# A hybrid attention block on one core: four group-norm scalings go from VectorE to ScalarE, and a retention preparation's query products come ahead of its key transposes

## The chip, the cores and the metric

The kernel runs on one core of a Trainium2 chip. The metric is the time of one execution on the device in microseconds, the median of several runs. Five engines work side by side, each through its own list of instructions in a fixed order: TensorE (PE: matrix products and transposes), VectorE (DVE), ScalarE (ACT), GpSimd (POOL) and SyncE (SP, which here issues DMA transfers). An engine whose next instruction waits for a semaphore holds everything that stands behind it in its list.

## The reference, cut to what matters

Two layers of a block with three branches (retention, neighborhood attention, latent attention), a gated merge and an MLP, over 512 tokens x and 256 context tokens z of width 1024. The change lies in the retention. There are four heads in two pairs, keys and queries of 64, values of 128, chunks of 128 tokens, and two directions:

```
qx, kx, vx = retention_qkv(px[0], px[1], px[2], rope)      # q and k rotated, k scaled
scores = einsum(qc, kc) * decay_mat                        # inside a chunk
inner  = einsum(scores, vc)
kv     = einsum(kc * k_decay, vc)                          # the state, chunk by chunk
cross  = einsum(qc * q_decay, s_prev)
o      = inner + cross                                     # for each direction

def head_group_norm(o, gain):                              # over the 128 of a head
    mu, var = mean(o), mean(square(o - mu))
    return merge_heads((o - mu) * rsqrt(var + EPS)) * gain

y = silu(g_fwd) * head_group_norm(o_fwd) + silu(g_bwd) * head_group_norm(o_bwd)
```

## The kernel before

All products are of fp32 split into a high and a low part, so that one product is three matrix products (L435, L436, L437 in the helper `mm3`; L656 to L658 with the tokens as output rows). The high part is copied by ScalarE (`hi_of`, L386), the low part is the difference that VectorE takes (`lo_of`, L389). A weight (`wsp`) is split in the same way when it has arrived from memory.

The branches are Python generators. `Retention.prep(p2)` prepares one pair of heads: it rotates the keys (`rotated("rk")`), makes values for the first two token tiles, transposes the keys back to tokens and scales them (`kt`, `ktf`), makes the decay matrices `gm` and `qd` by Exp on ScalarE, rotates the queries (`rotated("rq")`), makes the other values (`values(2)`, `values(4)`), then the states. A rotation is a product of 24 or 48 matrix instructions, a copy out of PSUM by ScalarE (L1229, tile `ra`; L1240, tile `rz`), four DMAs that swap halves of the partitions (L1232, `rb<-ra`), and three operations of VectorE (L1233 to L1235), after which `ra` is the rotated tensor.

`Retention.run(p2)` then goes over the items of the pair, one for each head and block of 256 tokens: six items in the first layer (context included), four in the second, for each of two pairs, so 20 in all. An item has three steps: s0 makes scores (L684) and multiplies them by `gm` (L1364, `pf`, split by L386 and L389); s1 multiplies by values and states (L1388 into the PSUM tiles `pst`), adds up (L1391 ScalarE, L1392 VectorE, tile `ro`) and does the group norm; s2 transposes the result (L1413) and scales it (L1418, `ry`). The group norm of an item is four statistics (L1398, L1399), an addition (L1400), a power by GpSimd (L1401, `rs`), four scalings (L1404) and the gates (L1405, L1406):

```
pool.tensor_tensor(rs, rs, half, op=ALU.pow)
for i in range(4):
    v = ov[:, i // 2, i % 2]
    dve.tensor_scalar(v, v, mv[:, i, 0:1], rs[:, i : i + 1], op0=ALU.subtract, op1=ALU.mult)
```

What a generator yields as it goes is woven into the steps of the loop that runs at the time (`fill.feed`): `prep(0)` into the neighborhood attention, `prep(1)` into `run(0)`, the branch outputs into `run(1)`. Behind this a scheduler puts each engine's instructions into one fixed list from its own estimate of when operands are there. PSUM tiles of the long products (`pd`) rotate through three banks, so that a product into a bank starts only when the tile that had it before has been read out.

In the profiled execution the retention of pair 0, with `prep(1)` woven in, runs from about 604 to 682 us in the first layer and from 2006 to 2068 us in the second. The neighborhood attention with `prep(0)` lies ahead of each, pair 1 at about 780 to 890 and 2110 to 2172 us.

Of the kernel before, what the change touches and what calls it, by code (L numbers as in the profile page):

```python
# [8 lines left out]
F32 = mybir.dt.float32  # L9
F32R = mybir.dt.float32r  # L10
BF16 = mybir.dt.bfloat16
AF = mybir.ActivationFunctionType
ALU = mybir.AluOpType
# [296 lines left out]
def cost(columns):  # L310

    return columns / 2400.0
# [3 lines left out]
def block_kernel(ctx, tc, xT, zT, cond, wu, sp, bias, tab, out):  # L316
# [11 lines left out]
    small = ctx.enter_context(tc.tile_pool(name="small", bufs=4))  # L328
# [8 lines left out]
    def nm(s):  # L337
        count[0] += 1
        return f"{s}_{count[0]}"
# [4 lines left out]
    def sgl(s="s"):  # L344
        return sgls.tile([128, 512], F32, tag="sgl", name=nm(s))
# [36 lines left out]
    act, dve, pool, pe, sync = nc.scalar, nc.vector, nc.gpsimd, nc.tensor, nc.sync  # L382
# [21 lines left out]
    for l in range(DEPTH):  # L404
        t = const.tile([128, SP_N], F32, name=f"sp{l}")
# [173 lines left out]
    def new_tiles(n, nk):  # L579

        r = []
        while len(r) < nk:
            r += halves(dbl("t"), n)
        return r[:nk]
# [579 lines left out]
    class Retention:  # L1164
# [39 lines left out]
        def prep(self, p2):  # L1204

            l, need, lg = self.l, self.need, self.lg
# [6 lines left out]
            dm, qp = dbl("dist"), sgl("qpos")  # L1213
# [44 lines left out]

            yield values(0)

            kt = new_tiles(512, 6)
            for src, i0 in ((k32, 0), (kz32, 4)):
                nt = src.shape[-1] // 128
# [9 lines left out]
                    hi_of(t[:, :256], f)  # L1273
                    lo_of(t[:, 256:], f, t[:, :256])
                yield cost(512)

            gm = new_tiles(512, 2)
            for o in range(2):
                for dr in range(2):
                    c = 4 * dr + 2 * p2 + o  # L1280
                    act.activation(gm[o][:, 256 * dr : 256 * dr + 256], dist[:, 256 * dr : 256 * dr + 256], AF.Exp, scale=lg[:, c : c + 1])

                ends, cut_off = (t.rearrange("p (e n) -> p e n", n=128)[:, 0:4:3] for t in (gm[o], mask))
                pool.tensor_tensor(ends, ends, cut_off, op=ALU.mult)

            qd = sgl("qd")
            for dr in range(2):
                act.activation(qd[:, 256 * dr : 256 * dr + 256], qp[:, 256 * dr : 256 * dr + 256], AF.Exp, scale=self.lq[:, p2, dr : dr + 1])
            qx, qz, q32, _ = rotated("rq", 1.0, need, False)
            yield cost(24 * (768 if need else 512))  # L1290
            for i in (2, 4):
                yield values(i)

# [49 lines left out]
        def item(self, p2, o, c):  # L1343
# [25 lines left out]
            def s1():  # L1369
                qx, qz, kx, kz, vs, gm, sts, qc = self.state[p2]  # L1370
                prob = st["p"]
                ops = [bank_t().rearrange("p (c h v) -> p c h v", c=2, h=2) for _ in range(2)]
                for ct in range(2):
                    for dr in range(2):

                        if dr == 0:
                            terms = [(0, 128 * ct)] + ([(1, 256)] if ct == 1 else [])
                        else:
                            terms = [(1, 128 * ct)] + ([(0, 256)] if ct == 0 else [])
                        mms = []  # L1380
                        for kt_i, col in terms:
                            v = vs[2 * c + kt_i][:, 256 * o : 256 * o + 256]
                            mms += [(t[:, col : col + 128], v) for t in prob[dr]]
                        if c < 2:
                            sv = sts[0 if (c == 0) == (dr == 0) else 1][dr]
                            mms.append((qc[o][dr][:, c0 + 128 * ct : c0 + 128 * ct + 128], sv[:, 256 * o : 256 * o + 256]))
                        for n, (a, b) in enumerate(mms):
                            pe.matmul(ops[dr][:, ct], R(a), R(b), start=n == 0, stop=n == len(mms) - 1)  # L1388
                ov = st["ov"] = sgl("ro").rearrange("p (c t v) -> p c t v", c=2, t=2)
                for dr in range(2):  # L1390
                    act.activation(ov[:, :, dr], ops[dr][:, :, 0], AF.Copy)  # L1391
                    dve.tensor_tensor(ov[:, :, dr], ops[dr][:, :, 1], ov[:, :, dr], op=ALU.add)  # L1392

                mv = small.tile([128, 4, 2], F32, tag="mv", name=nm("mv"))
                st6 = small.tile([128, 4, 6], F32, tag="st6", name=nm("st6"))
                rs = small.tile([128, 4], F32, tag="rs", name=nm("rs"))
                for i in range(4):
                    dve.bn_stats(st6[:, i], ov[:, i // 2, i % 2])  # L1398
                    dve.bn_aggr(mv[:, i], st6[:, i])  # L1399
                dve.tensor_scalar(rs, mv[:, :, 1], EPS, 0.0, op0=ALU.add, op1=ALU.add)  # L1400
                pool.tensor_tensor(rs, rs, half, op=ALU.pow)  # L1401
                for i in range(4):
                    v = ov[:, i // 2, i % 2]
                    dve.tensor_scalar(v, v, mv[:, i, 0:1], rs[:, i : i + 1], op0=ALU.subtract, op1=ALU.mult)  # L1404
                dve.tensor_tensor(ov, ov, st["gt"], op=ALU.mult)  # L1405
                dve.tensor_tensor(ov[:, :, 0], ov[:, :, 0], ov[:, :, 1], op=ALU.add)  # L1406

# [475 lines left out]
```

## Time and profile before

| what | value |
|---|---|
| median of 3 runs | 2614.82 us (2610.67 to 2619.2) |
| the profiled execution's own time | 2613.25 us |
| its span on the core | 2611.4 us |
| mean granted TensorE clock | 0.983 |
| PE busy | 2523.3 us (97%) |
| DVE busy | 1771.6 us (68%) |
| ACT busy | 1140.0 us (44%) |
| POOL busy | 135.6 us (5%) |

Busy is the time in which an engine has an instruction running, not the time in which it is the one that others wait for. The clock is the share of full speed that was granted to TensorE. The shares are means over the whole span; the stages of the retention look otherwise, and the windows and waits among the rows below show them by themselves.

### The profile page before, as it was taken

Reading aid. Unit: us, or ns where it says so; the run is one execution under the profiler, and the core shown is the slowest. Engines: PE = TensorE matmul, PEld = TensorE weight load, DVE = VectorE, ACT = ScalarE, POOL = GpSimd, SP = SyncE. Lnnn points to the kernel's source line nnn. Section 1 sums busy time; section 2 is a strip of 40 time slices with the busy share of each in tenths; the row PEclk is TensorE's granted clock in tenths of the full one; section 3 lists DMA queues with packets and bytes.
Section 4 is the critical chain, followed back from the end, with each engine's and each line's share of the span. In section 5 each row is a group of like instructions: output and inputs, shape, how many; then the busy total and the mean of one; then the engine's idle time right before and its main releaser. Section 6 shows DMA issues by size and latency. Waiting matters only on the chain.

```text
span 2611.4 us, 40080 instructions
## 1 busy us (share of the span) xinstructions
PE 2523.3 (97%) x15346; PEld 2246.8 (86%) x15346; DVE 1771.6 (68%) x3492; ACT 1140.0 (44%) x2144; POOL 135.6 (5%) x121
## 2 busy tenths in 40 slices
PE   8999999998999999999999999999999899999997
PEld 7999998998888877888888878889898788988887
DVE  6566556787979875666556767665668768744457
ACT  2555555564323345322222446554555434732325
POOL 0101000111000000000000000010001000000000
PEclk9899999999999999999999999999999999999999
DMA  6222224534765633344444424323554456433333
GB/s 242 92 71 89 69 86 127 156 92 138 255 196 157 205 112 104 121 133 142 127 132 129 143 79 140 97 82 104 148 158 116 129 184 204 145 98 97 97 97 121
DMA packets 151316, 340.46 MB, mean 130 GB/s; under 512 B 18642, under 2 KB 58962, under 8 KB 151124
## 3 DMA queue, kind: packets, MB, share of 16 engines
q1 hardware_dynamic: 140756, 322.17, 40.1%
q10 hardware_dynamic: 10368, 15.73, 1.6%
q8 instruction: 121, 1.98, 0.3%
q14 instruction: 71, 0.58, 0.1%
HBM read 288.27 MB, written 36.45 MB: 124 GB/s over the span
## 4 chain that ended last, share of the span: by engine, by line
PE 79%; DVE 10%; issue 3%; ACT 3%; DMA 2%; POOL 1%; SPq 1%; POOLq 0%; DVEq 0%; ACTq 0%
PE pd L437 20%; PE pd L436 20%; PE pd L435 20%; PE pso L625 3%; PE pst L608 3%; PE pd L658 3%; PE pd L656 3%; PE pd L657 3%; DVE op L389 1%; PE pss L436 1%; PE pss L435 1%; PE pss L437 1%; DVE wsp L389 1%; PE pss L684 1%; ACT wsp L386 1%
## 5 line engine op out<-in xcount | busy, mean ns | idle before, releaser
L435 PE MATMUL pd<-op,wsp 128*128 128x512 f32 (+1 forms) x3080 | 1072.3, 349 | 26.5 <-ACT op L597 5.9
L437 PE MATMUL pd<-op,wsp 128*128 128x512 f32 (+1 forms) x3080 | 1064.4, 347 | 11.7 <-DVE wsp L389 11.7
L436 PE MATMUL pd<-op,wsp 128*128 128x512 f32 (+1 forms) x3080 | 1070.0, 348 | 2.5 <-DVE op L389 2.3
L435 PEld LDWEIGHTS pd<-op,wsp 128*128 128x128 f32 x3080 | 587.7, 191 | 101.0 <-ACT wsp L386 7.1
L437 PEld LDWEIGHTS pd<-op,wsp 128*128 128x128 f32 x3080 | 587.2, 191 | 84.3 <-DVE wsp L389 14.1
L436 PEld LDWEIGHTS pd<-op,wsp 128*128 128x128 f32 x3080 | 588.9, 191 | 72.2 <-DVE op L389 6.5
L386 ACT ACTIVATE wsp<-wraw 128x1024 fp32r<-128x1024 f32 x319 | 336.4, 1055 | 431.8 <-PE pd L437 303.4
L389 DVE TENSOR_TENSOR wsp<-wraw,wsp 128x1024 fp32r<-128x1024 f32 x319 | 388.6, 1222 | 174.9 <-ACT wsp L386 174.0
L656 PE MATMUL pd<-wsp,op 128*128 128x256 f32 x704 | 202.1, 287 | 1.7 <-DVE pr L766 1.6
L658 PE MATMUL pd<-wsp,op 128*128 128x256 f32 x704 | 200.6, 285 | 0.9 <-DVE wsp L389 0.9
L657 PE MATMUL pd<-wsp,op 128*128 128x256 f32 x704 | 200.4, 285 | 0.0
L1770 DVE TENSOR_TENSOR rl<-rl 128x256 f32<-128x256 f32 (+1 forms) x104 | 59.0, 567 | 150.6 <-ACT rl L1769 150.4
L389 DVE TENSOR_TENSOR pt<-pst,pt 128x512 fp32r<-128x512 f32 (+1 forms) x208 | 121.7, 604 | 44.2 <-ACT pt L386 42.0
L1769 ACT ACTIVATE rl<-pd 128x256 f32<-128x256 f32 (+1 forms) x104 | 51.8, 499 | 227.4 <-PE pd L437 227.2
L1784 DVE TENSOR_TENSOR t<-pd,t 128x512 f32<-128x512 f32 (+1 forms) x132 | 81.0, 617 | 89.9 <-PE pd L437 89.5
L656 PEld LDWEIGHTS pd<-wsp,op 128*128 128x128 f32 x704 | 136.3, 194 | 2.7 <-issue 1.8
L658 PEld LDWEIGHTS pd<-wsp,op 128*128 128x128 f32 x704 | 136.1, 193 | 1.5 <-DVE wsp L389 1.5
L657 PEld LDWEIGHTS pd<-wsp,op 128*128 128x128 f32 x704 | 136.4, 194 | 0.0
L386 ACT ACTIVATE pt<-pst 128x512 fp32r<-128x512 f32 (+1 forms) x208 | 105.2, 529 | 50.9 <-PE pst L608 37.6
L625 PE MATMUL pso<-pt,t 128*128 128x256 f32 x704 | 115.5, 293 | 5.3 <-DVE tx L632 2.2
L512 DVE CUSTOM_DVE_ANT_0 cond<-graw,cond,sp 128x1024 bf16<-128x1024 f32 x80 | 102.4, 1280 | 17.4 <-DMA graw<-wu 17.1
L1445 ACT ACTIVATE gate<-pd 128x512 f32<-128x512 f32 x72 | 37.9, 527 | 165.1 <-PE pd L437 156.8
(273 smaller groups left out, 3441.4 us busy)
## 6 DMA issues: line engine op xcount, KB each, us to landing
wraw<-wu SPq DMA_DIRECT2D x327, 512.0 KB, 3.7
graw<-wu SPq DMA_DIRECT2D x56, 512.0 KB, 3.6
ada<-wu SPq DMA_DIRECT2D x40, 512.0 KB, 5.5
gg<-gate ACTq DMA_DIRECT2D x48, 256.0 KB, 2.0
gl<-gg SPq DMA_DIRECT2D x48, 256.0 KB, 3.6
zbias<-bias SPq DMA_DIRECT2D x64, 128.0 KB, 2.3
t<-vd SPq DMA_DIRECT2D x28, 256.0 KB, 5.4
gd<-gt SPq DMA_DIRECT2D x40, 128.0 KB, 2.5
```

Of the source, the lines that this page charges most:

```text
L386: act.activation(R(dst), src, AF.Copy, scale=scale)
L389: (eng or dve).tensor_tensor(R(dst), src, hi, op=ALU.subtract)
L435: pe.matmul(ps, R(a[0]), R(b[0]), start=start, stop=False)
L436: pe.matmul(ps, R(a[0]), R(b[1]), start=False, stop=False)
L437: pe.matmul(ps, R(a[1]), R(b[0]), start=False, stop=stop)
L512: i = dve.tensor_tensor_reduce(cs[2], raw, cs[t], 0.5, spt[l][:, SP_BADA + c : SP_BADA + c + 1], ALU.mult, ALU.add, mods[l][:, c, t : t + 1])
L608: pe.transpose(ps[:, 128 * k : 128 * k + 128], src[:, 128 * (a + k) : 128 * (a + k) + 128], ident)
L625: pe.matmul(o, R(vts[k]), R(pts[k]), start=k == 0, stop=k == n - 1)
L656: pe.matmul(ps, R(a[0]), R(w[0][:, o : o + 256]), start=k == 0, stop=False)
L657: pe.matmul(ps, R(a[1]), R(w[0][:, o : o + 256]), start=False, stop=False)
L658: pe.matmul(ps, R(a[0]), R(w[1][:, o : o + 256]), start=False, stop=k == nk - 1)
L1784: dve.tensor_tensor(a, ps, a, op=ALU.add)
```

## The change

In `prep`, the block that makes `gm` and `qd`, and the call of `rotated("rq")` with its yield, stand ahead of the block that transposes the keys; nothing in the blocks is altered. In the step s1 of an item, VectorE makes `shift`, minus the mean times `rs`, for the four norms at once, and the four scalings become ScalarE activations with `rs` as scale and `shift` as bias.

```
@@ prep @@
             yield values(0)
 
+            gm = new_tiles(512, 2)
+            for o in range(2):
+                for dr in range(2):
+                    c = 4 * dr + 2 * p2 + o
+                    act.activation(gm[o][:, 256 * dr : 256 * dr + 256], dist[:, 256 * dr : 256 * dr + 256], AF.Exp, scale=lg[:, c : c + 1])
+
+                ends, cut_off = (t.rearrange("p (e n) -> p e n", n=128)[:, 0:4:3] for t in (gm[o], mask))
+                pool.tensor_tensor(ends, ends, cut_off, op=ALU.mult)
+
+            qd = sgl("qd")
+            for dr in range(2):
+                act.activation(qd[:, 256 * dr : 256 * dr + 256], qp[:, 256 * dr : 256 * dr + 256], AF.Exp, scale=self.lq[:, p2, dr : dr + 1])
+            qx, qz, q32, _ = rotated("rq", 1.0, need, False)
+            yield cost(24 * (768 if need else 512))
+
             kt = new_tiles(512, 6)
             for src, i0 in ((k32, 0), (kz32, 4)):
...
                 yield cost(512)
-
...
-            qx, qz, q32, _ = rotated("rq", 1.0, need, False)
-            yield cost(24 * (768 if need else 512))
             for i in (2, 4):
                 yield values(i)
@@ item, s1 @@
                 pool.tensor_tensor(rs, rs, half, op=ALU.pow)
+                shift = small.tile([128, 4], F32, tag="sh", name=nm("sh"))
+                dve.scalar_tensor_tensor(shift, mv[:, :, 0], -1.0, rs, ALU.mult, ALU.mult)
                 for i in range(4):
                     v = ov[:, i // 2, i % 2]
-                    dve.tensor_scalar(v, v, mv[:, i, 0:1], rs[:, i : i + 1], op0=ALU.subtract, op1=ALU.mult)
+                    act.activation(v, v, AF.Identity, scale=rs[:, i : i + 1], bias=shift[:, i : i + 1])
                 dve.tensor_tensor(ov, ov, st["gt"], op=ALU.mult)
```

Line numbers move: the Exps from L1281 to L1265 and from L1288 to L1272, the transposes from L1266 to L1281, the scaled keys `ktf` from L1272 to L1287, the norms from L1404 to L1406, the gates from L1405 and L1406 to L1407 and L1408, the transposes of an item from L1413 to L1415. `shift` (tile `sh`) is L1403.

TensorE's list in the first layer, where `prep(1)` is woven into the first item, before the change. `pss` are scores, `pd` on L1266 the transposed keys; behind the last row stand 14 more rows of L1388 and then the first query product.

```order
L684 MATMUL pss_7444<-op_6487,op_6138 128x256
L1266 MATMUL pd_7310<-ctab,ra_7091 128x128 x4
L1266 MATMUL pd_7331<-ctab,rz_7106 128x128 x2
L1388 MATMUL pst_7265<-t_6261,pf_7123 128x256
L1388 MATMUL pst_7266<-t_6261,pf_7123 128x256
```

The same place after the change: the query products (`pd_7326`) follow the scores of the next item directly, and ten of them stand ahead of that item's products with the values.

```order
L684 MATMUL pss_7250<-op_6464,op_6145 128x256
L435 MATMUL pd_7326<-op_126,wsp_7323 128x512
L436 MATMUL pd_7326<-op_126,wsp_7323 128x512
L437 MATMUL pd_7326<-op_126,wsp_7323 128x512
L435 MATMUL pd_7326<-op_127,wsp_7323 128x512
```

And where the transposes of the keys stand after the change, behind all 48 query products and the next item's products; the rows on `pd_7511` begin `values(2)`.

```order
L1388 MATMUL pst_7431<-t_6262,pf_7256 128x256
L1415 MATMUL pso_7470<-ctab,ro_7153 128x128 x2
L1281 MATMUL pd_7479<-ctab,ra_7091 128x128 x4
L1281 MATMUL pd_7500<-ctab,rz_7106 128x128 x2
L684 MATMUL pss_7569<-op_6451,op_6138 128x256
L656 MATMUL pd_7511<-wsp_7181,op_126 128x256
```

So the wait for the rotated keys is no longer ahead of the query products in TensorE's list.

VectorE's list around the norm of the first item of the same layer, before:

```order
L1400 TENSOR_SCALAR rs_7160<-mv_7158 128x4
L1364 TENSOR_TENSOR pf_7255<-pss_7248,t_6411 128x256
L1404 TENSOR_SCALAR ro_7153<-ro_7153,mv_7158,rs_7160 128x128 x4
L389 TENSOR_TENSOR t_7187<-pd_7190,t_7187 128x2x128
L1405 TENSOR_TENSOR ro_7153<-ro_7153,gt_7006 128x512
```

After, with `shift` and, between it and the gate's product L1407, the four operations that VectorE has while ScalarE scales:

```order
L1400 TENSOR_SCALAR rs_7160<-mv_7158 128x4
L1364 TENSOR_TENSOR pf_7257<-pss_7250,t_6376 128x256
L1403 SCALAR_TENSOR_TENSOR sh_7171<-mv_7158,rs_7160 128x4
L389 TENSOR_TENSOR t_7189<-pd_7192,t_7189 128x2x128
L1364 TENSOR_TENSOR pf_7257<-pss_7250,t_6376 128x128
L1364 TENSOR_TENSOR pf_7262<-pss_7250,t_6376 128x256
L1364 TENSOR_TENSOR pf_7262<-pss_7250,t_6376 128x128
L1407 TENSOR_TENSOR ro_7153<-ro_7153,gt_7006 128x512
```

The four scalings have left VectorE's list, and the wait for `rs` is now that of `shift`.

ScalarE's list at the same place, before: splits of probabilities (`pf`) and values (`t`), and the sums of the next item (`ro_7283`).

```order
L386 ACTIVATE pf_7123<-pf_7130 128x384
L386 ACTIVATE t_7187<-pd_7190 128x2x128 x2
L386 ACTIVATE pf_7253<-pf_7255 128x384
L1391 ACTIVATE ro_7283<-pst_7265 128x2x128
L1391 ACTIVATE ro_7283<-pst_7266 128x2x128
L386 ACTIVATE pf_7253<-pf_7260 128x384
```

After:

```order
L386 ACTIVATE t_7189<-pd_7192 128x2x128 x2
L1406 ACTIVATE ro_7153<-ro_7153,sh_7171,rs_7160 128x128 x4
L386 ACTIVATE pf_7255<-pf_7257 128x384
L386 ACTIVATE pf_7255<-pf_7262 128x384
L1391 ACTIVATE ro_7285<-pst_7267 128x2x128
L1391 ACTIVATE ro_7285<-pst_7268 128x2x128
L1265 ACTIVATE t_7311<-dist_7031,lg_846 128x256 x4
L1272 ACTIVATE qd_7318<-qpos_7032,lq_867 128x256 x2
L1229 ACTIVATE ra_7376<-pd_7326 128x512
L386 ACTIVATE wsp_7829<-wraw_7827 128x1024
L1406 ACTIVATE ro_7285<-ro_7285,sh_7303,rs_7292 128x128 x4
L1240 ACTIVATE rz_7396<-pd_7351 128x256
```

The scalings (L1406) stand ahead of the next item's two splits, the six Exps have moved up, and the copies of the query product out of PSUM (L1229, L1240) stand behind Exps and, the second, behind the next item's scalings.

## Rows read from the trace of the kernel before

**Rows 1.** The page: busy time and share of the span, each engine.
```profile
PE 2523.3 (97%) x15346; PEld 2246.8 (86%) x15346; DVE 1771.6 (68%) x3492; ACT 1140.0 (44%) x2144; POOL 135.6 (5%) x121
```

**Rows 2.** Windows: length, busy PE, weight loads, DVE, ACT, POOL, granted clock, DMA.
```profile
530.00:604.00 74.00, 71.08 (x516) 66.06 (x515) 61.03 (x138) 48.08 (x112) 11.84 (x11) 1.00 0.37 109
604.00:682.00 78.00, 67.45 (x441) 61.48 (x441) 63.08 (x186) 32.18 (x71) 8.39 (x8) 0.93 0.42 129
...
780.00:890.00 110.00, 104.00 (x624) 91.24 (x623) 97.21 (x249) 33.23 (x60) 6.17 (x6) 1.00 0.61 190
1950.00:2006.00 56.00, 54.42 (x406) 51.05 (x405) 49.33 (x106) 36.13 (x79) 8.43 (x7) 1.00 0.36 101
2006.00:2068.00 62.00, 51.12 (x301) 44.14 (x300) 53.27 (x149) 29.39 (x62) 5.63 (x6) 0.88 0.35 96
...
2110.00:2172.00 62.00, 60.55 (x303) 50.69 (x302) 55.67 (x133) 20.32 (x32) 4.87 (x4) 1.00 0.66 214
```

**Rows 3.** Waits of PE, 604 to 682: total us, times, longest.
```profile
PE pd L1303 <- DVE t L389: 3.5, 2, 2.4
PE pd L1266 <- DVE ra L1235: 1.9, 1, 1.9
PE pss L684 <- DVE pf L1364: 1.9, 2, 0.9
```

**Rows 4.** Waits of PE, 2006 to 2068.
```profile
PE pd L1266 <- DVE ra L1235: 3.1, 1, 3.1
PE pd L435 <- ACT wsp L386: 2.7, 1, 2.7
```

**Rows 5.** The chain of waits, 650 to 682: shares by line.
```profile
by line: DMA ry<-ry 10.4%; DVE qc L1334 8.6%; DVE ro L1404 8.0%; DVE op L389 7.7%; DVE st L1398 6.5%; DVE ro L1405 5.6%; DVE st L389 5.3%; DVE pf L389 5.0%; DVE ro L1392 4.4%; DVE t L1316 4.1%; DVE ry L1418 3.5%; issue 3.4%; PE pd L435 3.0%
```

**Rows 6.** Timeline of PE, first layer: start, length, line, idle before and its end.
```profile
611.74 1.12 PE L684 MATMUL pss<-op,op 128*128 128x256 f32 x8
614.80 0.63 PE L1266 MATMUL pd<-ctab,ra 128*128 128x128 f32 x4 [1.94 <-DVE ra L1235]
...
616.56 1.55 PE L1388 MATMUL pst<-t,pf 128*128 128x256 f32 x3 [0.92 <-ACT pf L386]
...
621.21 0.76 PE L435 MATMUL pd<-op,wsp 128*128 128x512 f32 x1 [0.32 <-DVE t L389]
```

**Rows 7.** Timeline of PE, second layer, the same place.
```profile
2012.30 0.74 PE L684 MATMUL pss<-op,op 128*128 128x256 f32 x4 [0.52 <-DVE pf L1364]
2016.17 1.12 PE L1266 MATMUL pd<-ctab,ra 128*128 128x128 f32 x4 [3.14 <-DVE ra L1235]
...
2022.14 0.61 PE L435 MATMUL pd<-op,wsp 128*128 128x512 f32 x1
```

**Rows 8.** The chain of waits at 822: the sixteen products of an item at full clock.
```profile
822.66 1.91 PE pst L1388 x16
```

**Rows 9.** Timelines of ACT, SP's queue and DVE: the rotation of the keys, first layer.
```profile
604.74 0.58 ACT L1229 ACTIVATE ra<-pd 128x512 f32<-128x512 f32 x1
...
605.52 3.81 SPq L1232 DMA_DIRECT2D rb<-ra  x4
...
612.56 0.69 DVE L1233 TENSOR_TENSOR ra<-ra,rot 128x512 f32<-128x512 f32 x1 [3.73 <-DMA rb<-ra]
```

**Rows 10.** Line groups of the norm, whole trace: busy us, mean ns | idle before.
```profile
L1404 DVE TENSOR_SCALAR ro<-ro,mv,rs 128x128 f32<-128x128 f32 x80 | 22.3, 343 | 16.4 <-POOL rs L1401 16.4
...
L1400 DVE TENSOR_SCALAR rs<-mv 128x4 f32<-128x4 f32 x20 | 3.2, 162 | 0.1
```

**Rows 11.** Line groups of ACT, shapes apart: activations with two pointer operands.
```profile
L1567 ACT ACTIVATE t<-t,sp 128x256 f32<-128x256 f32 x24 | 14.2, 591 | 0.0
...
L1567 ACT ACTIVATE t<-t,sp 128x512 f32<-128x512 f32 x16 | 12.3, 805 | 0.0
```

**Rows 12.** Timeline of ACT, second layer's first preparation: four activations in a row.
```profile
1973.74 1.70 ACT L1281 ACTIVATE t<-dist,lg 128x256 f32<-128x256 f32 x4
```

**Rows 13.** Waits of PE, 780 to 890 (pair 1, first layer).
```profile
PE pd L435 <- DVE ms L1503: 3.6, 5, 1.2
```

More of the change, by code (lines that the diff above doesn't have):

```diff
@@ L1275, in prep @@
                 yield cost(512)
[L1277 to L1288, printed above, removed]
-            qx, qz, q32, _ = rotated("rq", 1.0, need, False)
-            yield cost(24 * (768 if need else 512))
             for i in (2, 4):
```

## The prediction

> **What bounds the kernel now.** First the page's busy times: TensorE works 97% of the span, VectorE 68%, ScalarE 44% [rows 1]. From that alone, taking work off VectorE and putting it on ScalarE would change nothing. So the second look goes to the windows, stage by stage, because the change touches only the retention. In the stages around it TensorE is nearly full (71.08 of 74 us, 54.42 of 56 us). In the two stages that run pair 0 it is not: 67.45 of 78 us in the first layer and 51.12 of 62 us in the second, so it stands idle for 10.55 and 10.88 us. There its granted clock is also below full speed, 0.93 and 0.88, so that part of its busy time is slow work [rows 2]. These two stages are where there is something to gain: 21.4 us of idle time, and by the clock up to 0.07 x 78 + 0.12 x 62 = 12.9 us.
>
> Third, who ends TensorE's waits there: VectorE nearly each time. The longest waits are for the split of the states' products (3.5 us), for `ra` at the key transposes (1.9 and 3.1 us) and for the products `pf` [rows 3, 4]. Fourth, the chain that ends last in the second half of the first layer's stage: its shares name line after line of VectorE, with the four scalings L1404 at 8.0%, and TensorE hardly at all [rows 5]. In these stages VectorE's list, busy 63.08 of 78 us and 53.27 of 62 us [rows 2], with its waits for other engines, sets when TensorE may go on.
>
> **The key transposes.** In the first layer the scores end at 611.74 + 1.12 = 612.86 us, and the first query product starts at 621.21 us, 8.35 us later [rows 6]. In between TensorE does six transposes and 16 products L1388. At full clock those 16 take 1.91 us [rows 8], 0.119 us for one of 256 columns, and six transposes of half that size about 0.4 us (an estimate from the same row). So 8.35 - 1.91 - 0.4 = 6.0 us are lost to waits (1.94, 0.92 and 0.32 us are named) and to work at half speed. In the second layer it is 2022.14 - 2013.04 = 9.10 us, so 6.8 us lost [rows 7]. The cause lies far ahead: the copy of the keys is done at 605.3 us, the four DMA issues take 3.81 us on SP's queue, and VectorE gets the swapped half only at 612.56 us, after 3.73 us of idle time [rows 9]. The query products need none of this, only x and a weight. After the change they stand directly behind the scores; in the first layer they are 24 of 512 and 24 of 256 columns, 24 x 0.239 + 24 x 0.119 = 8.6 us by row 8, longer than the 1.94 us by which `ra` was late. The stall at this place should go: 6.0 and 6.8 us at most.
>
> **What is late next.** The query copies L1229 and L1240 must empty their PSUM banks. In ScalarE's new list they stand behind Exps and the scalings of an item, so `values(2)`, which takes over such a bank, can wait for them; and `values(4)` takes over a bank of the transposed keys, and waits for VectorE's fourth `ktf`, which is now made only after the late transposes. Before, the transposed keys had their bank emptied long ahead. No row shows these waits. Below, they are nothing, where 48 products of 0.119 us cover them; above, from the two places in the lists, about 1.5 us for the first and 3 us for the second, 4.5 us in one preparation. The transposes also delay the states at the end of `prep`, whose work on VectorE is on the chain [rows 5]. No transfer is added; the queries' swap DMAs now start earlier, and I price that at nothing, as only VectorE's query rotation waits for them.
>
> **The scalings.** On VectorE one costs 343 ns and four of an item 1.11 us as they overlap; the new `shift` has four columns, and I price it as L1400, 162 ns [rows 10]. Net relief of VectorE: 0.95 us an item. On ScalarE the trace has activations with two pointer operands only for 256 columns (591 ns) and 512 (805 ns) [rows 11], 0.84 ns a column, so 128 columns give 591 - 107 = 484 ns. Four activations of 496 ns take 1.70 us in a row, so each starts 0.40 us after the one ahead [rows 12]; four of 484 ns then take about 484 + 3 x 390 = 1.65 us. The item's own chain therefore gets longer, by 0.16 + 1.65 - 1.11 = 0.7 us plus a change of engine. That costs nothing where VectorE has 1.65 us of other work between `shift` and the gate's product; in the new list it has that in about 14 of 20 items (in the first item of the first layer four operations), and in the others I expect waits of 0.6 to 1.1 us. ScalarE has room: 32.18 of 78 and 29.39 of 62 us busy [rows 2]. The wait for GpSimd's power (16.4 us over 20 items) [rows 10] stays; it is now `shift` that waits.
>
> Here the Trainium skill speaks against the change: "ScalarE: Activation LUTs", section "Rules for kernel authors", says to put plain multiplies and additions on VectorE and not on ScalarE. By the engine time of one operation the trace agrees (484 against 343 ns); whether that decides the kernel's time is the third case below. The same page, section "What ACT_TABLE_LOAD costs", gives 186 ns plus 93 ns for each pointer operand plus 0.833 ns a column, an estimate of 479 ns here, 386 ns in a row and 1.64 us for four; the sum would be the same by it, since the trace's extrapolation comes to 1.65 us.
>
> **The sum.** First layer, 604 to 682 us: five items' scalings lie in it, 5 x 0.95 = 4.75 us off VectorE, which sets the end of the stage. Of the 6.0 us at the transposes I count a third, about 2.2 us: TensorE's earlier products help only as far as VectorE's list gets its input sooner by them, and its last 30 us follow its own work. Together -7 us; bounds: -1.5 (the stall goes, 4.5 us of bank waits come, and the relief is lost in waits for ScalarE) and -10.8 (all of both). Second layer, 2006 to 2068 us: 4 x 0.95 = 3.8 us and a third of 6.8 us, -6 us; bounds -2.3 and -10.6. Pair 1 (ten items): TensorE is idle 6.0 us of 110 and 1.45 of 62 [rows 2], 3.6 us of it for VectorE's `ms` of the branch outputs [rows 13], which stand among the items' work; I take -1.5 us, between 0 and -3. The preparations of pair 0 lie in stages where TensorE is idle for only 2.9 and 1.6 us [rows 2], so nothing is to be had and the bank waits can come: +2 us, between 0 and +4.5. Sum: -7 - 6 - 1.5 + 2 = -12.5 us, with bounds of -24 and +1. The profiled execution took 2613.25 us, 1.6 us below the median of the runs, so 2600.75, about 2601 us.
>
> **Rivals.** What a measurement can tell from no change is about 0.3%, 7.8 us: faster is below 2607, slower above 2622.7.
>
> *The waits take each other's place.* TensorE leaves the transposes' stall only to stand at `values(2)` and `values(4)`, and VectorE, which is the bound, loses part of its relief in waits for ScalarE. For it speak the three banks and the late place of the copies; against it that TensorE's list has other work to do first. Relief of 9 x 0.95 = 8.6 us less 4.5 us of new waits: about -4 us, 2609 us, no change to be told. Chance 0.25.
>
> *ScalarE's list becomes the path.* The scalings stand in it ahead of the next item's two splits of `pf`, and they wait for VectorE's `shift`, thus for GpSimd. If those splits come late, the products L1388 do, and VectorE's low parts. An item then loses 0.7 us, plus a split that stands behind (an estimate of 0.55 us from its 384 columns between those of rows 11 with no pointers), 1.25 us: 20 x 1.25 - 12.8 (the stalls) = +12 us, 2625 us. It decides from (12.8 + 7.8)/20 = 1.0 us an item on. Against it: ScalarE is busy for less than half of these stages, and most items have cover. This is where the quoted rule of the Trainium skill would lead. Chance 0.12.
>
> *Much more comes back.* With fewer gaps the granted clock rises too; most of the 21.4 us of idle time and of the 12.9 us of slow clock return, about -28 us, 2585 us. Against it: the waits for states' splits (3.5 us) and weights (2.7 us) [rows 3, 4] are not touched. Chance 0.04.
>
> **The numbers.** The forecast has 0.59, with its own range of 2594 to 2608 us. To leave out no more than 2 in 10, the range reaches over the first rival and to the lower bound of the sum: 2588 to 2615 us. Faster: nearly all of the forecast and the last rival, 0.58; same: the first rival and the forecast's edge, 0.29; slower: the second rival and a little of the first, 0.13.
>
> **What the next profile would show.** Right: no wait of TensorE for `ra` at L1281; query products directly behind the scores at about 613 and 2013 us at full clock; the granted clock of both stages above 0.93 and 0.88; `shift` instead of the norm waiting for GpSimd, about 16 us in all; scalings of about 0.48 us on ScalarE, four in 1.65 us; waits of VectorE at the gate's product L1407 of no more than some 6 us. The forecast is wrong if L656 (`values`) waits for L1229, L1240 or `ktf` by more than 4 us a preparation, if the gate's product waits in most items, or if the two stages of pair 0 get shorter by less than 4 us each although the stall is gone: then VectorE's chain, not TensorE's stall, held the time.

## The result and the profile after

| | before | after |
|---|---|---|
| median | 2613.76 us (6 runs) | 2600.02 us (6 runs, 2595.34 to 2602.31) |
| ratio of the runs | 1 | 0.9948, 95% interval 0.9938 to 0.9957 |
| profiled execution: own time, span | 2613.25, 2611.4 us | 2601.97, 2600.2 us |

The forecast was 2601 us, faster. One execution of a later run took 6331.56 us where its others took 2589 to 2600 us; it is left out of that run's ratio. The page's first part of the changed kernel answers to [rows 1]:

```profile
PE 2520.1 (97%) x15346; PEld 2246.1 (86%) x15346; DVE 1749.7 (67%) x3432; ACT 1170.3 (45%) x2224; POOL 135.9 (5%) x121
```

VectorE is 21.9 us less busy, ScalarE 30.3 us more. The line groups of the norm, as [rows 10] gave them for before (busy us, mean ns | idle before and what ended it):

```profile
L1406 ACT ACTIVATE ro<-ro,sh,rs 128x128 f32<-128x128 f32 x80 | 33.0, 483 | 49.1 <-DVE sh L1403 49.1
...
L1407 DVE TENSOR_TENSOR ro<-ro,gt 128x512 f32<-128x512 f32 x20 | 13.8, 689 | 3.7 <-ACT ro L1406 2.8 <-DMA rb<-ra 0.5
...
L1403 DVE SCALAR_TENSOR_TENSOR sh<-mv,rs 128x4 f32<-128x4 f32 x20 | 3.3, 163 | 18.4 <-POOL rs L1401 18.4
```

The extrapolated prices held: 483 ns for a scaling (484 had been worked out) and 163 ns for `shift` (162). The wait for GpSimd went from the norm to `shift`, and the gate's product L1407 waits for ScalarE in 4 of the 20 items, 2.8 us in all. The two stages of pair 0, beside [rows 2]:

```profile
604.00:675.00 71.00, 63.95 (x443) 59.21 (x443) 57.86 (x171) 40.01 (x91) 7.18 (x8) 0.98 0.45 133
...
2000.00:2060.00 60.00, 50.36 (x300) 44.39 (x299) 51.16 (x141) 34.76 (x78) 5.79 (x6) 0.89 0.42 122
```

In the first layer TensorE's clock is 0.98 in place of 0.93. In the second it is 0.89 in place of 0.88, hardly better, and TensorE is still idle for 9.64 of 60 us; 2.8 us of that is the wait of L435 for a split weight (L386), which was 2.7 us before [rows 4]. TensorE's timeline at the old stall, beside [rows 6], and its later waits in the same stage:

```profile
613.30 0.64 PE L684 MATMUL pss<-op,op 128*128 128x256 f32 x4
613.78 0.40 PE L435 MATMUL pd<-op,wsp 128*128 128x512 f32 x1
...
627.43 0.60 PE L1281 MATMUL pd<-ctab,ra 128*128 128x128 f32 x4
...
629.24 0.39 PE L656 MATMUL pd<-wsp,op 128*128 128x256 f32 x1 [0.87 <-ACT rz L1240]
...
642.23 0.58 PE L656 MATMUL pd<-wsp,op 128*128 128x256 f32 x1 [3.06 <-DVE ktf L1287]
```

The query products follow the scores at once, and L1281 waits for nothing here (in the second layer it waits 1.1 us for a split, L389, and not for `ra`). Later `values(2)` waits 0.87 us for a copy by ScalarE, and `values(4)` 3.06 us for the scaled keys: the two new bank waits that the prediction priced at no more than 1.5 and 3 us. Why the copy is late stands in ScalarE's timeline, where L1240 comes behind Exps and two items' scalings:

```profile
620.30 1.65 ACT L1406 ACTIVATE ro<-ro,sh,rs 128x128 f32<-128x128 f32 x4 [1.05 <-DVE sh L1403]
...
623.31 1.70 ACT L1265 ACTIVATE t<-dist,lg 128x256 f32<-128x256 f32 x4
624.91 0.90 ACT L1272 ACTIVATE qd<-qpos,lq 128x256 f32<-128x256 f32 x2
625.71 0.58 ACT L1229 ACTIVATE ra<-pd 128x512 f32<-128x512 f32 x1
...
627.27 1.65 ACT L1406 ACTIVATE ro<-ro,sh,rs 128x128 f32<-128x128 f32 x4
628.83 0.36 ACT L1240 ACTIVATE rz<-pd 128x256 f32<-128x256 f32 x1
```

**Where the time came from.** GpSimd's power stands once in every item, so its start is a mark at the same place of both programs. First and last item of pair 0 in each layer, before and then after (timeline of GpSimd):

```profile
618.57 1.01 POOL L1401 TENSOR_TENSOR rs<-rs,half 128x4 f32<-128x4 f32 x1 [18.07 <-DVE rs L1400]
...
680.35 1.85 POOL L1401 TENSOR_TENSOR rs<-rs,half 128x4 f32<-128x4 f32 x1 [14.90 <-DVE rs L1400]
...
2020.30 1.01 POOL L1401 TENSOR_TENSOR rs<-rs,half 128x4 f32<-128x4 f32 x1 [20.73 <-DVE rs L1400]
...
2053.05 1.01 POOL L1401 TENSOR_TENSOR rs<-rs,half 128x4 f32<-128x4 f32 x1 [5.00 <-DVE rs L1400]
```

```profile
619.06 1.01 POOL L1401 TENSOR_TENSOR rs<-rs,half 128x4 f32<-128x4 f32 x1 [17.15 <-DVE rs L1400]
...
674.57 1.82 POOL L1401 TENSOR_TENSOR rs<-rs,half 128x4 f32<-128x4 f32 x1 [13.72 <-DVE rs L1400]
...
2010.70 1.01 POOL L1401 TENSOR_TENSOR rs<-rs,half 128x4 f32<-128x4 f32 x1 [20.55 <-DVE rs L1400]
...
2039.37 1.01 POOL L1401 TENSOR_TENSOR rs<-rs,half 128x4 f32<-128x4 f32 x1 [3.56 <-DVE rs L1400]
```

At 411 us both profiles are still equal but for 0.8 us (first L1082: 411.2, then 410.4). The last item of pair 0 is 5.8 us early, so the neighborhood attention with `prep(0)` and pair 0 gained 5.0 us together. How they share it hangs on the mark that is put between them. By the first item, which is 0.5 us late, the attention lost 1.3 us and pair 0 gained 6.3, but part of the old stall lies ahead of that mark [rows 6]. Pair 1 of that layer ends 7.1 us early (842.51, 835.45): another 1.3. The work behind it, which the change does not touch, brings 1.2 (last L916, in the second layer: 1821.5, 1813.2, 8.3 us early). In the second layer the last item of pair 0 is 13.7 us early, so attention and pair 0 gained 5.4 us there. By the first item (9.6 us early) the attention has 1.3 us of this and pair 0 4.1; by the attention's last L1082 (1985.7, 1978.2, 7.5 us early) the attention lost 0.8 us and pair 0 gained 6.2. Pair 1 ends 16.3 us early (2153.47, 2137.16), 2.6 us more.

The end is only 11.2 us early. The branch outputs behind pair 1 of the second layer give back 2.6 us (from 2200 us on, the starts of like instructions lie 13.7 us apart in the median), and 3.3 us are lost at about 2240 us, in layer norms that the change does not touch; behind these another 0.8 us comes back. The windows there (after, then before) show TensorE about as busy, but at another clock. In the first of them TensorE also waits 0.9 us for GpSimd (L739 for L1539), a wait that the kernel before does not have:

```profile
2226.00:2247.00 21.00, 17.63 (x116) 16.36 (x115) 15.88 (x38) 14.71 (x29) 0.90 (x1) 0.84 0.35 106
```

```profile
2240.00:2260.00 20.00, 17.33 (x135) 16.27 (x135) 16.76 (x37) 16.13 (x32) 0.00 (x0) 1.00 0.41 128
```

The profiled execution took 2601.97 us; another of the six took 2595.34 us, with a mean clock of 0.987 in place of 0.983.

### The profile page after: what moved, and what is told of

Read it like the earlier page. It is cut to its first block, busy times and chain, and to the rows that moved or that the text cites. A ratio compares the mean times of both kernels' runs of the same rounds, so it can differ in the third digit from the quotient of the medians.

```text
span 2600.2 us, 40112 instructions
## 1 busy us (share of the span) xinstructions
PE 2520.1 (97%) x15346; PEld 2246.1 (86%) x15346; DVE 1749.7 (67%) x3432; ACT 1170.3 (45%) x2224; POOL 135.9 (5%) x121
## 4 chain that ended last, share of the span: by engine, by line
PE 80%; DVE 9%; issue 4%; ACT 3%; DMA 2%; POOL 1%; SPq 0%; POOLq 0%; ACTq 0%; DVEq 0%
PE pd L437 20%; PE pd L436 19%; PE pd L435 19%; PE pd L656 3%; PE pd L658 3%; PE pd L657 3%; PE pso L625 3%; PE pst L608 3%; DVE op L389 1%; DVE wsp L389 1%; PE pss L436 1%; PE pss L437 1%; PE pss L435 1%; PE pss L684 1%; DMA gl<-gg 1%
## 5 line engine op out<-in xcount | busy, mean ns | idle before, releaser
L435 PE MATMUL pd<-op,wsp 128*128 128x512 f32 (+1 forms) x3080 | 1071.5, 349 | 20.9 <-ACT wsp L386 5.6
L435 PEld LDWEIGHTS pd<-op,wsp 128*128 128x128 f32 x3080 | 587.9, 191 | 93.8 <-ACT wsp L386 7.2
L386 ACT ACTIVATE wsp<-wraw 128x1024 fp32r<-128x1024 f32 x319 | 336.3, 1055 | 396.0 <-PE pd L437 271.9
L389 DVE TENSOR_TENSOR wsp<-wraw,wsp 128x1024 fp32r<-128x1024 f32 x319 | 388.7, 1222 | 171.7 <-ACT wsp L386 168.7
L656 PE MATMUL pd<-wsp,op 128*128 128x256 f32 x704 | 204.7, 291 | 7.2 <-DVE ktf L1287 3.7
L658 PE MATMUL pd<-wsp,op 128*128 128x256 f32 x704 | 202.2, 288 | 0.5 <-DVE wsp L389 0.5
L657 PE MATMUL pd<-wsp,op 128*128 128x256 f32 x704 | 202.4, 288 | 0.0
L389 DVE TENSOR_TENSOR pt<-pst,pt 128x512 fp32r<-128x512 f32 (+1 forms) x208 | 121.7, 603 | 42.7 <-ACT pt L386 40.8
L656 PEld LDWEIGHTS pd<-wsp,op 128*128 128x128 f32 x704 | 138.3, 197 | 9.3 <-DVE ktf L1287 4.1
L658 PEld LDWEIGHTS pd<-wsp,op 128*128 128x128 f32 x704 | 138.1, 196 | 1.0 <-DVE wsp L389 1.0
L657 PEld LDWEIGHTS pd<-wsp,op 128*128 128x128 f32 x704 | 138.4, 197 | 0.0
L386 ACT ACTIVATE pt<-pst 128x512 fp32r<-128x512 f32 (+1 forms) x208 | 105.3, 529 | 52.7 <-PE pst L608 38.3
```

What stands on the lines that cost most here:

```text
L386: act.activation(R(dst), src, AF.Copy, scale=scale)
L389: (eng or dve).tensor_tensor(R(dst), src, hi, op=ALU.subtract)
L435: pe.matmul(ps, R(a[0]), R(b[0]), start=start, stop=False)
L656: pe.matmul(ps, R(a[0]), R(w[0][:, o : o + 256]), start=k == 0, stop=False)
L657: pe.matmul(ps, R(a[1]), R(w[0][:, o : o + 256]), start=False, stop=False)
L658: pe.matmul(ps, R(a[0]), R(w[1][:, o : o + 256]), start=False, stop=k == nk - 1)
```

## The experiments

Theory 1 is the prediction's: VectorE's list sets the end of the stages, so its relief brings most of the gain and the stall at the transposes little by itself. Theory 2: the stall was what counted. All ratios are to runs of before on the same chip, with their 95% interval; times "against the change" are worked out from the two ratios times 2613 us, and the two intervals together leave 3 to 5 us either way on such a difference. Every edit lets the scheduler write all lists anew from there on; they are not otherwise held fixed. So a run shows its edit together with the lists that came of it.

### One half at a time

The first run has only the preparation's order (the first part of the diff), the second only the scalings (the second part).

> Only the preparation is reordered; the four scalings stay on VectorE. By the prediction's sum (theory 1: VectorE's list sets the end of the two stages, the stall at the key transposes gives back only a third) the gain is 2.2 + 2.2 us in the pair 0 stages, less up to 2 us of new bank waits in the neighborhood attention: 0 to -5 us, about 2611 us, with the waits of values(4) for the keys' scaling and no wait of TensorE for ra. By the rival (theory 2: TensorE's stall was what counted) nearly all of the change's 14 us comes with it: -9 to -14 us, 2600 to 2605 us.

> Only the four scalings go to ScalarE; the preparation keeps its order. Theory 1: VectorE is relieved of 0.95 us an item and that is most of the gain, -8 to -11 us, 2603 to 2606 us, with TensorE's wait for ra at the key transposes still there (1.9 and 3.1 us before). Theory 2: little, 0 to -4 us, since the stall is still there.

Order alone: 0.9998 (0.9989 to 1.0006), -0.5 us. Scalings alone: 0.9961 (0.9949 to 0.9973), -10.2 us. Both: -13.6 us. Theory 2 is out, since it had 9 to 14 us for the order alone. TensorE's waits of that run, 604 to 690 us, show that no wait for `ra` is left, and what came in its place:

```profile
PE pd L656 <- DVE ktf L1287: 4.3, 1, 4.3
PE pso L1413 <- DVE ry L1418: 2.7, 1, 2.7
PE pd L435 <- ACT gate L1445: 2.0, 1, 2.0
PE pd L656 <- ACT rz L1240: 1.8, 1, 1.8
```

and the window at the end of that stage:

```profile
670.00:680.00 10.00, 4.80 (x15) 3.15 (x14) 9.01 (x25) 3.37 (x7) 1.01 (x1) 0.72 0.88 288
```

TensorE had its products done earlier, ran out of them, and stood idle for 5.2 of 10 us at a clock of 0.72 while VectorE was busy for 9.01; of these 5.2 us it waited 2.7 for VectorE's `ry`, 2.0 for a gate of ScalarE and 0.5 for a split. In this layer the stall was thus not removed but moved to the end of the stage, where VectorE has work left: the last item of pair 0 comes 3.0 us earlier than before, the first of pair 1 4.2 us later (GpSimd's power at 677.34 and 785.79 us, before 680.35 and 781.56). In the second layer it went otherwise: the last item of pair 0 comes 6.3 us later than before and the first of pair 1 only 0.2 us later (2059.37 and 2117.84, before 2053.05 and 2117.69). Why is open.

With the scalings alone the wait for `ra` is still there (1.4 us in the first, 3.4 us in the second layer), and the gain as well. On top of them the order brings another 3.4 us by the ratios, with 4 us either way, so this is not clear of noise.

### VectorE's time given back

```
                     act.activation(v, v, AF.Identity, scale=rs[:, i : i + 1], bias=shift[:, i : i + 1])
+                for i in range(5):
+                    dve.tensor_scalar(spare, ident[:, :64], rs[:, i % 4 : i % 4 + 1], 1.0, op0=ALU.mult, op1=ALU.add)
```

> The change with five operations of VectorE an item added that nothing reads (64 columns of a constant, scaled by rs, so they come behind the power as the four scalings did). ScalarE's scalings stay, and no data hangs on the added work; by the rows of 128 and of 4 columns (343 and 162 ns, four of 128 columns in 1.11 us) five take about 1.0 to 1.3 us, as much as the change took off VectorE. Theory 1 (the length of VectorE's list is the path): what the scalings' move gained goes, about +9 to +14 us against the change. Rival (the gain came from the item's data taking another way, not from VectorE's free time): less than +4 us.

0.9982 (0.9973 to 0.9990): 8.9 us slower than the change. The group of the added operations, with their busy time:

```profile
L1409 DVE TENSOR_SCALAR spare<-ctab,rs 128x64 f32<-128x64 f32 x100 | 24.8, 248 | 0.4
```

Nothing waits for them, yet 24.8 us of VectorE's time cost 8.9 us, just under the 9 to 14 us of theory 1 and clear of the rival's 4: the length of VectorE's list costs time without any data that hangs on it, about a third of what was added. By the marks 5.7 us of it fall in pair 0 of the first layer (first and last item at 618.67 and 679.85 us, in the change at 619.06 and 674.57).

### ScalarE's scalings left out, and made longer

The first leaves out the four activations (the outputs stay unscaled); the others cut each into two or four pieces of columns.

```
-                    act.activation(v, v, AF.Identity, scale=rs[:, i : i + 1], bias=shift[:, i : i + 1])
+                    for e in range(0, 128, 64):          # 32 for the quarters
+                        act.activation(v[:, e : e + 64], v[:, e : e + 64], AF.Identity, scale=rs[:, i : i + 1], bias=shift[:, i : i + 1])
```

> The change without the four scalings, on either engine: the norm's outputs are left unscaled (statistics, power and shift are still made). Taking the 1.65 us of ScalarE out of an item's chain shows what they still cost where they are. If they are covered, as the prediction has it for 14 of 20 items with 0.6 to 1.1 us in the others: 0 to -6 us against the change. If ScalarE's part is a new path of its own: -10 us or more.

> The change with every scaling cut into two of 64 columns: eight activations an item in place of four, about 7 x 0.34 + 0.43 = 2.8 us in place of 1.65, 1.1 us longer an item. The run with quarters, 3.4 us longer an item, lost 15.5 us, or 0.23 us for each us of ScalarE in an item. In proportion this would be +5 us; if there is a threshold at the cover of about 1.65 us that the prediction named, little is lost below it and the loss is 0 to +3 us; if already the first 1.1 us fall on a place without cover, as GpSimd's extra operation did in another run (+10 us), +8 us or more.

> The change with every scaling cut into four of 32 columns: 16 activations an item in place of 4. From the rows of before (591 and 805 ns for 256 and 512 columns, 0.40 us apart for 256) one of 32 columns takes about 400 ns and follows the one ahead after about 0.31 us, so an item's scalings take about 5.0 us in place of 1.65, 3.4 us longer. If ScalarE's scalings are covered by VectorE's other work (theory 1), an item loses only what exceeds its cover: 1 to 2 us for 20 items on the path in part, +10 to +30 us against the change and waits of the gate's product for ScalarE in most items. If ScalarE had so much room that the place does not matter at all (a rival), less than +5 us. If the item's chain is the path throughout, 20 x 3.4 = +68 us.

Left out: 0.9956 (0.9942 to 0.9969), no gain over the change (+2 us, within both intervals). In the total, the 1.65 us of ScalarE an item cost nothing that can be measured. That every item is covered does not follow: in this run the last item of the first layer's pair 0 comes 3.4 us earlier than in the change (671.19, 674.57), and what was gained is lost right behind it, where TensorE waits for VectorE (1.9 us for `ry`, 1.4 us for a split) and then runs at a low clock. The windows there (left out, then the change):

```profile
670.00:680.00 10.00, 8.21 (x24) 6.43 (x25) 9.03 (x16) 0.00 (x0) 1.85 (x1) 0.66 0.96 338
```

```profile
670.00:680.00 10.00, 10.00 (x58) 8.72 (x58) 9.01 (x25) 4.99 (x10) 1.82 (x1) 1.00 0.99 373
```

Halves: 0.9990 (0.9981 to 0.9999), +11 us. Quarters: 1.0011 (1.0002 to 1.0019), +16.5 us, slower than before. So the cover ends right behind what the change uses: the first 1.1 us more an item cost 11 us, the next 2.3 another 5.5 us. The gate's product of the halves (line group):

```profile
L1408 DVE TENSOR_TENSOR ro<-ro,gt 128x512 f32<-128x512 f32 x20 | 13.8, 690 | 12.2 <-ACT ro L1407 11.6 <-DMA gl<-gg 0.4
```

It waits 12.2 us in place of 3.7. That is 8.5 of the 11 us; the rest is within the intervals. In the same stage TensorE's wait for the copy of the query product (L656 for L1240) lasts 2.7 us in place of 0.9, and its wait for L1392 at the last item but one 3.7 us in place of 1.9. The 8 us behind this second wait are (halves, then the change)

```profile
662.10:670.10 8.00, 7.99 (x32) 6.80 (x33) 6.99 (x24) 4.40 (x13) 1.01 (x1) 0.79 0.05 16
```

```profile
657.60:665.60 8.00, 7.96 (x43) 6.75 (x44) 6.98 (x25) 4.36 (x10) 1.01 (x1) 1.00 0.14 51
```

In the quarters the bank wait that the prediction named is the largest of the stage, 5.8 us for a copy that stands behind 16 activations:

```profile
PE pd L656 <- ACT rz L1240: 5.8, 1, 5.8
PE pst L1388 <- DVE ro L1392: 5.6, 1, 5.6
```

### Shift on GpSimd

```
+                dve.tensor_scalar(shift, mv[:, :, 0], -1.0, 0.0, op0=ALU.mult, op1=ALU.add)
                 pool.tensor_tensor(rs, rs, half, op=ALU.pow)
+                pool.tensor_tensor(shift, shift, rs, op=ALU.mult)
```

> The change with shift made on GpSimd: VectorE makes minus the mean ahead of the power, and GpSimd multiplies it by rs behind the power, so that VectorE no longer stands waiting for GpSimd (16.4 us over 20 items before, 18.4 us after the change). The item's chain gets longer by GpSimd's second operation, about 1 us, as long as its power. Theory 1 (VectorE's list is the path, an item's own chain has cover): a gain of up to 0.9 us an item where VectorE stood, about -4 to -10 us against the change. Rival (the item's chain is the path): +1 us an item in the two pair 0 stages, +5 to +10 us.

0.9989 (0.9981 to 0.9998), +10.7 us: theory 1 as it stood in this expectation failed, and the time is that of its rival, for which the item's chain is the path (+5 to +10 us). The line groups of GpSimd's product and of the gate's:

```profile
L1404 POOL TENSOR_TENSOR sh<-sh,rs 128x4 f32<-128x4 f32 x20 | 8.3, 417 | 1.6
```

```profile
L1408 DVE TENSOR_TENSOR ro<-ro,gt 128x512 f32<-128x512 f32 x20 | 13.8, 692 | 28.9 <-ACT ro L1407 28.8
```

VectorE no longer waits at `shift`, but at the gate's product, for 28.9 us in place of 18.4 + 3.7 = 22.1 us: in 19 of 20 items that product stands in its list ahead of the time at which the scaling is done. This is 6.8 of the 10.7 us. The mistake was to take a wait off VectorE's list without anything that moves its next reader. What counts is VectorE's time and waits together, not its instructions alone.

### The transposes later, the Exps later

The first moves the block of the key transposes behind `values(2)` and `values(4)`; the second leaves the six Exps behind the transposes.

```
             qx, qz, q32, _ = rotated("rq", 1.0, need, False)
             yield cost(24 * (768 if need else 512))
+            for i in (2, 4):
+                yield values(i)
             kt = new_tiles(512, 6)
...
-            for i in (2, 4):
-                yield values(i)
```

> The change with the block that transposes the keys moved on, behind values(2) and values(4), so that values(4) no longer takes over the bank of the transposed keys (3.1 us of waiting in the first layer's pair 0 stage). If those waits cost what they last, -3 to -5 us. If VectorE's list sets the end of the stage, its scaled keys, which the states need, come later by about two times 5.7 us of products, and the waits go to the products of the states: 0 to +6 us.

> The change with the block of the six Exps left behind the key transposes, so that only the query products and their rotation move ahead. In ScalarE's list the copies L1229 and L1240, which empty the banks of the query products, then stand in front of the Exps. If the waits of values(2) for these copies (0.9 us in the first layer, 0.8 us in the second) come from the Exps ahead of them, they go and the kernel gains 0 to 2 us against the change; the second copy still stands behind an item's scalings. If the Exps' early place matters for the items (the decay matrices gm come late), a loss of 2 to 5 us.

Transposes later: 1.0048 (1.0035 to 1.0060), 26 us slower than the change, where no more than 6 us had been expected. The wait of `values(4)` is gone, but the scaled keys and states that VectorE makes from the transposes, and the decayed queries that stand behind them in its list, come at the very end. TensorE waits 6.1 us for `pf` in the first layer's stage and runs 660 to 670 us at half clock:

```profile
660.00:670.00 10.00, 7.17 (x27) 6.12 (x28) 8.07 (x28) 6.21 (x18) 1.16 (x1) 0.50 0.00 0
```

Exps later: 0.9953 (0.9940 to 0.9965), no difference that can be told from the change.

### More off VectorE

```
-                dve.tensor_scalar(dst, ps, spt[self.l][:, SP_GN + h : SP_GN + h + 1], 0.5, op0=ALU.mult, op1=ALU.mult)
+                act.activation(dst, ps, AF.Copy, scale=spt[self.l][:, SP_GN + h : SP_GN + h + 1])
```

The factor 0.5 is multiplied into the gains once, at the start. The edit was run on the change, on the change with the later Exps, and on the run with the scalings alone.

> The change with one more operation taken off VectorE: the scaled copy of an item's transposes out of PSUM (ry, about 0.38 us, 20 items) is made by ScalarE. Theory 1 (VectorE's list is the path, at 8.9 us of time for 24.8 us of added busy time in the run with spare operations, so 0.36 us for each): 20 x 0.4 = 8 us off VectorE give -2 to -4 us against the change. Rival (what is left is set by ScalarE's order and the chain of an item, as the halves' +11 us suggest): 0 to +8 us.

> The two edits of the runs beside it together: the Exps behind the key transposes, and ry on ScalarE. If each does what its first case says, -3 to -6 us against the change, about 2595 us; if the effect of each hangs on where the lists happen to leave TensorE idle, the sum doesn't hold, by 4 us or more.

> The scalings and ry on ScalarE, with the preparation in its old order. Against the run with the scalings alone (0.9961 of before, -10 us): theory 1 gives another -2 to -4 us; if ScalarE's list or the item's chain is the path, 0 to +8 us.

On the change: 0.9934 (0.9919 to 0.9949), -3.7 us, by itself not clear of noise. On the scalings alone: 0.9940 (0.9929 to 0.9952), -5.5 us. With the later Exps: 0.9908 (0.9894 to 0.9921), a median of 2589.02 us, the fastest version found, 10.5 us under the change. All three are faster, as theory 1 has it, but only the first has its size: 20 operations of 467 ns, 9.3 us, are off VectorE, 2 to 4 us were expected, and with the later Exps the edit brings 11.8 us, more than the time that was moved. The sum of the two edits, -3.7 and +1.3, does not hold; it is 8 us better, with 7 us either way. TensorE's waits of the fastest version in the second layer's stage (1995 to 2060 us) show what is left:

```profile
PE pss L685 <- DMA op<-op: 1.6, 1, 1.6
PE pd L437 <- DVE wsp L389: 1.2, 1, 1.2
PE pd L657 <- DVE t L389: 0.7, 1, 0.7
```

and its window, then that of the change:

```profile
2000.00:2055.00 55.00, 50.91 (x312) 45.36 (x312) 49.35 (x134) 36.31 (x81) 6.41 (x6) 0.97 0.43 125
```

```profile
2000.00:2055.00 55.00, 45.36 (x279) 40.28 (x278) 47.77 (x134) 33.88 (x76) 5.79 (x6) 0.88 0.37 100
```

The 8 us are thus mostly of the second layer, where gaps and slow clock go together. The marks put them behind the last item of pair 0: there the fastest version is 1.2 us ahead of the change (2038.20, 2039.37), at the first item of pair 1 9.3 us (2093.92, 2103.25), and in between the change waits 2.8 us for a split weight (L435 for L386), the fastest version not at all. Which of the moved instructions does it there was not tried. Lists written anew can thus be worth as much as an edit itself, so the direction of the runs together carries the argument, and the size of one run alone does not.

## Why the prediction was right

**What bounds the stages.** VectorE's list, as the chain of waits had it [rows 5]. Taking the scalings off it (-10.2 us), giving it spare work (+8.9) and taking `ry` off it (-3.7, -5.5, -11.8) all move the time the way this has it. The share of 68% over the span [rows 1] did not show it; the windows did. What the prediction had too simply is the list itself: its waits for an item's chain through GpSimd and ScalarE count like its work, as the run with `shift` on GpSimd and the halves show (+10.7 and +11 us).

**The scalings.** Relief of 0.95 us an item was the term, 4.75 + 3.8 + 1.5 = 10 us of the sum; 10.2 us were measured alone, with 3 us either way. The price on ScalarE held to 1 ns, which by the row for 256 columns was an extrapolation. That they are mostly covered shows in the gate's product, which waits 2.8 us in all; leaving them out gains nothing in the total. How thin the cover is, the prediction had only in part: it expected 0.6 to 1.1 us in each of six items, and 1.1 us more an item took most of the gain away.

**The transposes.** Up to 6.0 and 6.8 us are lost there [rows 6, 7]. The prediction counted a third of it, a share that no row gave: 4.4 us, less 2 us of new waits in the attention, 2.4 us. Measured are 3.4 us on top of the scalings and 0.5 us alone, with 4 and 2 us either way. So it is small, as forecast, but the third itself is not shown. That TensorE's stall returns only as far as VectorE's list ends sooner fits the first layer of the run with the order alone; its second layer is not explained. The new waits lay where they were expected: 0.9 us for L1240, 3.1 us for `ktf`, 0.8 us for L1229 in the second layer, against 1.5 and 3 us as an upper bound. With the order alone those for L1240 and `ktf` were above it, 1.8 and 4.3 us. In the attention only 0.6 us of such a wait is seen (for `ktf`, first layer).

**By stages.** Attention and pair 0 together: 2 - 7 - 6 = -11 us forecast, -5.0 and -5.4 us measured by the marks. Pair 1: -1.5 us forecast, -1.3 measured in the first layer, and in the second -2.6 that the branch outputs behind it give back. That is -11.7 us where the change acts; the places that it does not touch add 0.5 us (-0.8, -1.2, +3.3, -0.8), which makes the 11.2 us of the two profiles. That the median of 2600.02 us lies within 1 us of the forecast is in part luck: places without an edit moved by about 1 to 3 us, and the six executions spread over 7 us.

**The rivals.** ScalarE's list as the path was priced to begin at 1.0 us an item. Nothing of it is seen in the change, but it is near: the halves, 1.1 us longer, came to 0.9990, and the quarters were slower than before. The rule of the Trainium skill quoted there, multiplies and additions on VectorE ("ScalarE: Activation LUTs", "Rules for kernel authors"), is right about one operation's time in this trace (483 against 343 ns) and would have decided wrongly here, where VectorE is the engine that is waited for. That the waits take each other's place is what the order does alone. Of the rival in which most of the idle time and of the slow clock comes back, little is seen: TensorE is still idle for 7.05 of 71 and 9.64 of 60 us, and in the second layer the clock stayed at 0.89. One price in the prediction does not come from where it says: [rows 11] have no activation without pointer operands, so the 0.55 us for a split is in none of them. The trace of before has 0.52 us for it (L386 on `pf`, 128x384), which leaves that rival's sum as it was.

## What to carry to other kernels

Look for the engine whose list ends last in the stage, not over the span, and move work off that engine even to one that is slower at it, as long as the receiver's time lies beside other work of the first; measure the cover by making the moved work longer, since it can end within 1 us. A stall of TensorE that is filled with other products may only be moved when another engine's list sets the end of the stage, as in the first layer here. Where every edit has all lists written anew, follow marks that both programs have through the whole trace, since a stage can gain what the next one loses. In a fixed list, taking away a wait without moving its next reader moves the wait to that reader.

## What the runs showed of the hardware that was not expected

A short wait can be followed by a stretch at a lower clock. In the first layer's stage the 8 us behind the wait for L1392 ran at a granted clock of 1.00 where the wait was 1.9 us (the change), and at 0.79 where it was 3.7 us (the halves) and 2.9 us (the spare operations). But it is not the length of this one wait alone: with the scalings alone it was 2.6 us, and the clock behind it 0.65. A window behind waits for `pf` ran at 0.50, the lower of the two levels (1.2 of 2.4 GHz). The clock also differs far from the edits: 0.84 against 1.00 over some 20 us in a layer norm, 3.3 us of a profiled execution, about as much as the order of the preparation is worth. A new wait of 0.9 us for GpSimd lies there, but other runs without it have 0.84 there too (the fastest version), so what decides it is open. And GpSimd's product of 128x4 took 417 ns where its power of the same size takes 1.0 us; its expectation had counted 1 us.
